# Moving the S5 and merge arithmetic of a two-layer diffusion trunk from GpSimd to VectorE, with branch products in their own PSUM tile

## The chip, the cores and the metric

The kernel runs on one core of one Trainium2 chip. The metric is the device time of one execution in microseconds; the median of three runs of the kernel before is 2266.82 us (2264.76 to 2268.28).

The engines are named as in the profile: PE is TensorE's matmul, PEld its weight load, DVE is VectorE, ACT is ScalarE, POOL is GpSimd, SP is SyncE, whose queue issues all DMAs of this kernel.

## What is computed

Two layers over 512 latent tokens and 256 context tokens, width 1024. Each layer normalises its input, projects it with one wide matrix, feeds four mixers, and merges them:

```python
hx = _rmsnorm(x, p["norm_g"]) * (1.0 + scale_x) + shift_x
zx = _project(hx, p["w_in"], ALL_NAMES)
# four mixers: S5 (complex diagonal scan, GLU), short convolution,
# neighbourhood attention, grouped-query attention
for k, (name, y) in enumerate(zip(BRANCH_NAMES, ys)):
    gated = y * jax.nn.silu(z[name + "_gate"])
    contrib = jax.nn.sigmoid(z["merge_" + name]) * (gated @ p["w_br"][k])
    out = contrib if out is None else out + contrib
x_new = x + gate_x * (out @ p["w_out"])
```

The first layer carries context and latent tokens (768 columns, in the code two parts, "c" of 256 and "l" of 512); the second layer's outputs are wanted for the 512 latent tokens alone. The S5 mixer has 32 groups of 16 channels, 64 complex states each, run forwards and backwards.

## The kernel before

Activations lie with features on the 128 partitions and tokens along the free dimension. A dense product (`dense`, line 187) splits weights and activations into a rounded high part and a low rest, and makes three matmuls per tile: high by high, high by low, low by high. `unit` (line 164) loads a weight unit of 128x1024, casts the high parts on ACT (line 177) and subtracts for the low parts (line 178); `lo_eng` gives that subtraction to POOL and DVE in turn. Raw weights have 2 buffers, high and low halves 4 each, which is two units.

Each layer has two stages. `front` weaves attention tiles with projections, the convolution and gates. `back` merges the branches in the order convolution, neighbourhood attention, grouped-query attention, S5. In `merge`, for each of 8 output tiles m of a branch, `merge_z` makes the sigmoid's product (8 k-tiles) and its tanh (line 1293, tile `mt`, 3 buffers in layer one and 2 in layer two), and a second `dense` makes the branch's product from `gh` and `gl` (4 k-tiles), the gated branch output reloaded from DRAM (line 1304). DVE combines both (line 1325); POOL adds the result to the accumulator (lines 1330, 1327). Both products use the PSUM tiles `pl` (2 buffers) and `pc` (1 buffer). The sigmoid of m+1 is emitted ahead of the branch product of m.

During the first three merges `tick` emits the S5 work of 8 blocks of 4 groups from a plan with due times (`s5_plan`). A block has:

- `s5_factors`: from a table of powers (`skl`) and the layer's matrices it makes `sX` (six small operations, lines 1012 to 1017), and per direction `swin` on DVE (512 columns) and `sWO` on POOL (576 columns), each of three operations at lines 1030 to 1032
- `s5_phases` (layer one only): six operations on 768 columns, lines 965 to 970; ACT negates the result at line 971
- `s5_matrices`: transposes and small products on PE (lines 1049, 1058)
- `s5_states`: a rotation (lines 1143 to 1145, two products and an add), the scan (1147), a rotation back (1150, 1151) and differences (1155 to 1158). Before each rotation the halves are swapped by DMAs (lines 1141, 1148). One of the two products is on POOL (1144, 1151)
- `s5_outputs` on PE (lines 1173 to 1175)

During the S5 merge and the output products of layer one, `s5_ahead` makes the factors and matrices of the first `n_ahead // 4` blocks of layer two, stores them to DRAM, and layer two loads them. The rest is made in layer two.

Instructions of each engine run in the order that the scheduler wrote them in at build time: by priority, which is program order except for weight units and attention tiles, and by when its own model of time has them ready. So later work can stand ahead of earlier work that waits.

Of the kernel before, what the change touches and what calls it, by code (L numbers as in the profile page):

```python
# [11 lines left out]
F32 = mybir.dt.float32  # L12
# [25 lines left out]
SG = 4  # L38
# [84 lines left out]
class Net:  # L123
# [63 lines left out]
    def dense(self, w, k0, nk, xh, xl, parts, base=0, turn=0):  # L187
# [485 lines left out]
    def front(self, l, pool, parts):  # L673

        self.attention_constants(pool)
# [109 lines left out]
    K_PR, K_PI, K_BR, K_AR, K_BI, K_AI, K_FR, K_FI, K_RHO, K_N = 0, 9, 18, 26, 38, 46, 58, 59, 60, 61  # L785
    NE = 2 * SG

    def s5_prep(self, pool):
# [147 lines left out]
        self.pd = self.tc.dram_tile([32 // SG, 128, self.K_N * self.NE], F32, name="pd")  # L936
        for c in range(32 // SG):
            R = pool.tile([128, self.K_N, self.NE], F32, name="skt", bufs=2)
            e = slice(c * self.NE, (c + 1) * self.NE)
            for col, t, w in ((self.K_PR, pr, 9), (self.K_PI, pi, 9), (self.K_FR, fr, 1), (self.K_FI, fi, 1), (self.K_RHO, rho, 1),  # L940
                              (self.K_BR, br_, 8), (self.K_BI, bi_, 8), (self.K_AR, ar_, 12), (self.K_AI, ai_, 12)):
                nc.scalar.copy(R[:, col:col + w], t[:, :w, e] if w > 1 else t[:, None, e])
            nc.sync.dma_start(self.pd[c], R.rearrange("p k e -> p (k e)"))
# [3 lines left out]
    def s5_table(self, l, pool, g0):  # L947

        K = pool.tile([128, self.K_N, self.NE], F32, name="skl", bufs=2)
        for h in range(2):  # L950
            self.nc.sync.dma_start(K[64 * h:64 * h + 64].rearrange("p k e -> p (k e)"), self.pd[g0 // SG][64 * l:64 * l + 64])
        return K

    def s5_phases(self, pool, prep, g0):
# [4 lines left out]
        P = prep.tile([128, self.K_N, self.NE], F32, name="skl", bufs=2)  # L959
        nc.sync.dma_start(P.rearrange("p k e -> p (k e)"), self.pd[g0 // SG])  # L960
# [31 lines left out]
    def s5_factors(self, l, pool, out, g0, bufs):  # L992
# [3 lines left out]
        P = self.s5_table(l, pool, g0)  # L996
# [13 lines left out]
        fr, fi = (P[:, c, :, None].to_broadcast([128, self.NE, 16]) for c in (self.K_FR, self.K_FI))  # L1010
# [8 lines left out]
        def powered(out, d, k0, k1, desc, m1, m2, w):  # L1019

            E = V if w == 8 else G

# [427 lines left out]
```

## Time and profile before

| | us |
|---|---|
| median of 3 runs | 2266.82 |
| the profiled execution, whole | 2275.09 |
| its span, first to last instruction | 2273.3 |
| PE busy | 2132.0 (94%) |
| DVE busy | 1308.9 (58%) |
| ACT busy | 891.7 (39%) |
| POOL busy | 818.7 (36%) |

The profiled execution is 8.3 us over the median of the runs. The stages, read from the lines at work: front of layer one to about 678 us, back of layer one to about 1300, front of layer two to about 1837, back of layer two to the end. A busy share says nothing of which wait ends last; the rows below are read by stage, and of each wait the releaser is named. PEclk is the share of TensorE's full clock that was granted: 1.0 is 2.4 GHz, and 0.5, its only other level here, 1.2 GHz.

### The profile page before, as it was taken

The numbers are of one execution on the slowest core, as the hardware profiler recorded it, in microseconds if no ns is written. First come the engines' busy times: TensorE is split into PE (matmuls) and PEld (weight loads), VectorE is DVE, ScalarE is ACT, GpSimd is POOL, SyncE is SP. The second block draws the span as 40 slices with busy tenths as digits, with TensorE's granted clock in tenths as the row PEclk, the third lists the DMA queues.
The fourth block names the chain that finished last, engine by engine and source line by source line (L and its number), as shares of the span: only waits on it lengthen the run. The fifth ranks groups of instructions, "written<-read, shape, count | busy, mean of one in ns | idle before, by whom it ended". The sixth has DMA issues, their size and how long they took to land.

```text
span 2273.3 us, 34769 instructions
## 1 busy us (share of the span) xinstructions
PE 2132.0 (94%) x12868; PEld 1817.7 (80%) x12868; DVE 1308.9 (58%) x2466; ACT 891.7 (39%) x1936; POOL 818.7 (36%) x630
## 2 busy tenths in 40 slices
PE   8999999999997989989999999999999979888999
PEld 3788888888986877778887897888788868777877
DVE  6477675688647667865337533555446644465322
ACT  3454454446442322222334235555445533223332
POOL 1712122222314436554247423222323333474332
PEclk9999999999998989999999989999999989988999
DMA  6454454433225453453255635444423357644344
GB/s 243 126 154 131 113 174 130 129 102 103 95 87 163 136 163 107 127 168 107 67 191 167 203 119 193 110 121 124 142 84 105 96 144 208 199 121 132 122 130 138
DMA packets 163470, 310.94 MB, mean 137 GB/s; under 512 B 58594, under 2 KB 82402, under 8 KB 162532
## 3 DMA queue, kind: packets, MB, share of 16 engines
q1 hardware_dynamic: 163300, 308.72, 44.8%
q8 instruction: 101, 1.65, 0.3%
q14 instruction: 69, 0.57, 0.1%
HBM read 211.33 MB, written 48.55 MB: 114 GB/s over the span
## 4 chain that ended last, share of the span: by engine, by line
PE 43%; DVE 6%; DMA 5%; issue 3%; SPq 3%; POOL 2%; ACT 1%; DVEq 0%; ACTq 0%; POOLq 0%
PE pl L204 29%; PE pc L204 5%; PE M L594 2%; DMA s<-s 1%; PE T L585 1%; DMA gl<-gd 1%; SPq L1067 1%; PE T L1058 1%; PE S L558 1%; DMA s<-yd 1%; PE S L560 1%; PE M L473 1%; DVE swin L1030 0%; DMA gd<-s 0%; PE T L1132 0%
## 5 line engine op out<-in xcount | busy, mean ns | idle before, releaser
L204 PE MATMUL pl<-hh,whi 128*128 128x512 f32 x1312 | 533.1, 408 | 23.1 <-ACT whi L177 10.1
L204 PE MATMUL pl<-hh,wlo 128*128 128x512 f32 x1312 | 531.0, 405 | 11.0 <-DVE wlo L178 6.5
L178 POOL TENSOR_TENSOR wlo<-wraw,whi 128x512 fp32r<-128x512 f32 x220 | 311.6, 1420 | 636.3 <-ACT whi L177 555.7
L204 PE MATMUL pl<-hl,whi 128*128 128x512 f32 x1312 | 531.2, 405 | 0.0
L177 ACT CAST whi<-wraw 128x512 fp32r<-128x512 f32 x440 | 271.3, 619 | 541.7 <-PE pl L204 242.5
L204 PEld LDWEIGHTS pl<-hh,whi 128*128 128x128 f32 x1312 | 253.8, 194 | 76.9 <-ACT whi L177 11.0
L204 PEld LDWEIGHTS pl<-hh,wlo 128*128 128x128 f32 x1312 | 252.9, 193 | 67.3 <-DVE wlo L178 8.5
L204 PEld LDWEIGHTS pl<-hl,whi 128*128 128x128 f32 x1312 | 253.6, 193 | 51.9 <-DVE hl L225 0.6
L178 DVE TENSOR_TENSOR wlo<-wraw,whi 128x512 fp32r<-128x512 f32 x220 | 181.8, 829 | 163.6 <-ACT whi L177 162.7
L204 PE MATMUL pc<-hh,whi 128*128 128x256 f32 x768 | 227.2, 296 | 13.8 <-DVE mt L1325 5.8
L204 PE MATMUL pc<-hl,whi 128*128 128x256 f32 x768 | 223.5, 291 | 0.8 <-DVE hl L225 0.8
L204 PE MATMUL pc<-hh,wlo 128*128 128x256 f32 x768 | 222.5, 290 | 0.0
L204 PEld LDWEIGHTS pc<-hh,whi 128*128 128x128 f32 x768 | 149.9, 195 | 23.2 <-DVE mt L1325 6.7
L574 ACT ACTIVATE s<-s,stiny 128x512 f32<-128x512 f32 (+2 forms) x160 | 112.5, 703 | 111.9 <-DVE stiny L573 55.7
L204 PEld LDWEIGHTS pc<-hl,whi 128*128 128x128 f32 x768 | 149.9, 195 | 5.8 <-DVE hl L225 1.8
L204 PEld LDWEIGHTS pc<-hh,wlo 128*128 128x128 f32 x768 | 149.9, 195 | 0.3
L594 PE MATMUL M<-ph,v 128*64 128x128 f32 x1216 | 146.3, 227 | 3.3 <-ACT y L612 1.4
L204 PE MATMUL pl<-gh,whi 128*128 128x512 f32 x256 | 106.3, 415 | 31.0 <-DMA gh<-gd 20.1
L594 PEld LDWEIGHTS M<-ph,v 128*64 128x64 f32 x1216 | 126.3, 137 | 10.9 <-ACT y L612 2.8
L224 ACT CAST ph<-T 128x512 fp32r<-128x512 f32 (+2 forms) x192 | 92.6, 496 | 57.0 <-PE T L585 50.0
L479 POOL TENSOR_TENSOR qtiny<-qtiny,kc 128x12 f32<-128x12 f32 (+1 forms) x26 | 56.0, 2155 | 140.3 <-DVE qtiny L477 113.0
L204 PE MATMUL pl<-gl,whi 128*128 128x512 f32 x256 | 104.2, 407 | 2.4 <-DMA gl<-gd 2.4
(785 smaller groups left out, 4230.9 us busy)
## 6 DMA issues: line engine op xcount, KB each, us to landing
wraw<-wu SPq DMA_DIRECT2D x220, 512.0 KB
wada<-wada SPq DMA_DIRECT2D x40, 512.0 KB
s<-s SPq DMA_DIRECT2D x80, 192.0 KB
bias<-bias SPq DMA_DIRECT2D x64, 128.0 KB
kh<-qhi SPq DMA_DIRECT2D x40, 192.0 KB
kl<-qlo SPq DMA_DIRECT2D x40, 192.0 KB
gh<-gd SPq DMA_DIRECT2D x16, 384.0 KB
gl<-gd SPq DMA_DIRECT2D x16, 384.0 KB
```

The costliest lines, as they stand in the source:

```text
L177: nc.scalar.copy(hi, raw[:, c])
L178: e.tensor_tensor(lo, raw[:, c], hi.bitcast(F32), op=OP.subtract)
L204: mm = nc.tensor.matmul(out[q], a[:, c], b[k][:, s], start=k + n == 0, stop=k == nk - 1 and n == 2)
L224: self.nc.scalar.copy(hi, src)
L473: nc.tensor.matmul(sums[:, 2 * b:2 * b + 2], sq[:, c:c + 128], self.blk1, start=True, stop=True)
L479: nc.gpsimd.tensor_tensor(r[:, :2 * nb], t[:, :2 * nb], self.mhalf.to_broadcast([128, 2 * nb]), op=OP.pow)
L558: nc.tensor.matmul(S[:, 512 - n:512], qa, k[:, CTX + k0 * 64:CTX + k0 * 64 + n], start=i == 0, stop=i == 1)
L560: nc.tensor.matmul(S[:, 512:768], qa, k[:, :CTX], start=i == 0, stop=i == 1)
L574: nc.scalar.activation(s[:, a:e], s[:, a:e], AF.Exp, bias=tn[:, 1:2], accum_out=tn[:, 2:3])
L585: nc.tensor.transpose(T[:, (b - b0) * 128:(b - b0 + 1) * 128], s[:, a + b * 128:a + (b + 1) * 128], self.ident)
L594: last = nc.tensor.matmul(o[:64, :128], v[:, vb, w], p[:, c], start=i == 0, stop=i == 3 * nb - 1)
L1058: nc.tensor.matmul(o[:16, g * 128:(g + 1) * 128], X[:, 0, d, g], WO[:, d, g, d:d + 8].rearrange("p k i -> p (k i)"), start=True, stop=True)
```

## The change

- `lo_eng` gives the low halves to POOL and DVE in turn only in the front stages; in the back stages all go to DVE.
- `sWO`, the second product of both S5 rotations, and the accumulator's adds go from POOL to DVE.
- The table of powers lies per column with the powers contiguous, so that an operation reads them at a step of one element and not of eight; the radius column goes to its end.
- The branch product of `merge` goes to the PSUM tile `S` (1024 columns, one buffer), which the attention tiles use in the front stages.
- The sigmoids come from one list for all branches, and up to three are held. Of the S5 branch only the first may come before its merge starts.
- `n_ahead` is 32: all 8 blocks of layer two are made in layer one.
- In layer two `mt` has 3 buffers, `gh` and `gl` have 2, and the pool for making weights is gone.

```diff
     @property
     def lo_eng(self):
         self._n = getattr(self, "_n", 0) + 1
-        return self.nc.gpsimd if self._n % 2 else self.nc.vector
+        return self.nc.gpsimd if self._n % 2 and self.in_front else self.nc.vector
...
-                if q not in out:
+                if wide is not None:
+                    out[q] = wide[:, 512:512 + s.stop - s.start] if q == "c" else wide[:, :512]
+                elif q not in out:
...
-        A = lambda c: P[:, c:c + 12].rearrange("p a e -> p e a")[:, :, :, None].to_broadcast([128, self.NE, 12, 8])
-        B = lambda c: P[:, c:c + 8].rearrange("p b e -> p e b")[:, :, None, :].to_broadcast([128, self.NE, 12, 8])
+        A = lambda c: P[:, :, c:c + 12, None].to_broadcast([128, self.NE, 12, 8])
+        B = lambda c: P[:, :, None, c:c + 8].to_broadcast([128, self.NE, 12, 8])
...
-            E = V if w == 8 else G
...
-            E.tensor_tensor(out, pw(self.K_PR), mm(m1), op=OP.mult)
-            E.tensor_tensor(tp, pw(self.K_PI), mm(m2), op=OP.mult)
-            E.tensor_tensor(out, out, tp, op=OP.add)
+            V.tensor_tensor(out, pw(self.K_PR), mm(m1), op=OP.mult)
+            V.tensor_tensor(tp, pw(self.K_PI), mm(m2), op=OP.mult)
+            V.tensor_tensor(out, out, tp, op=OP.add)
...
-        G.tensor_tensor(xs, xs, S, op=OP.mult)
+        V.tensor_tensor(xs, xs, S, op=OP.mult)
...
-        G.tensor_tensor(gs, gs, S, op=OP.mult)
+        V.tensor_tensor(gs, gs, S, op=OP.mult)
...
-    n_ahead = 24
+    n_ahead = 32
...
-            if (br, m) not in self.mz:
-                self.merge_z(l, br, m, parts)
-            if m < 7:
-                self.merge_z(l, br, m + 1, parts)
-            elif after is not None:
-                self.merge_z(l, after, 0, parts)
+            ahead = [x for x in self.zs if x[0] != B_S5 or x[1] == 0 or br == B_S5]
+            for x in ahead[:max(0, 3 - len(self.mz))]:
+                self.zs.remove(x)
+                self.merge_z(l, *x, parts)
...
-            b = self.dense(w, 4 * (m % 2), 4, gh, gl, parts, self.base)
+            wide = self.ps.tile([128, 1024], F32, name="S")
+            b = self.dense(w, 4 * (m % 2), 4, gh, gl, parts, self.base, wide=wide)
...
-                nc.gpsimd.tensor_tensor(t, acc[m], t, op=OP.add)
+                nc.vector.tensor_tensor(t, acc[m], t, op=OP.add)
...
-                nc.gpsimd.tensor_tensor(acc[m], acc[m], t, op=OP.add)
+                nc.vector.tensor_tensor(acc[m], acc[m], t, op=OP.add)
...
+            self.ngh = 2 if last else 1
+            prep = None if last else stack.enter_context(tc.tile_pool(name=f"s5p_{l}", bufs=1, reuse_waits="tile"))
...
-                net.nmt, net.mz = (3, 2)[l], {}
+                net.nmt, net.mz = 3, {}
```

## Rows read from the trace of the kernel before

**Rows 1.** Busy time by stretch, the two back stages; columns: window, length, engines, PEclk, DMA
```profile
678.50:1300.00 621.50, 566.39 (x3273) 486.33 (x3273) 390.90 (x467) 183.36 (x358) 301.80 (x202) 0.95 0.49 145
...
1837.40:2273.30 435.90, 392.16 (x1793) 319.51 (x1792) 189.46 (x223) 126.65 (x234) 180.74 (x135) 0.95 0.51 152
```

**Rows 2.** The same view, finer: the first back stage's start and its S5 blocks
```profile
678.50:700.00 21.50, 8.91 (x30) 7.12 (x30) 14.76 (x13) 2.51 (x6) 8.98 (x7) 0.68 0.78 259
700.00:1100.00 400.00, 364.10 (x2111) 313.84 (x2110) 267.75 (x311) 114.22 (x225) 191.90 (x130) 0.94 0.47 131
```

**Rows 3.** Waits of PE, first back stage: us in total, times, longest
```profile
PE pl L204 <- DMA gh<-gd: 12.6, 1, 12.6
PE pl L204 <- ACT whi L177: 10.1, 3, 4.5
PE T L1174 <- DVE s L1155: 6.8, 2, 3.8
PE pc L204 <- DVE mt L1325: 5.8, 2, 5.1
```

**Rows 4.** Waits of PE, second back stage
```profile
PE T L1058 <- POOL sWO L1032: 10.2, 2, 5.6
PE pl L204 <- DMA gh<-gd: 7.5, 2, 6.4
PE pl L204 <- ACT mt L1293: 7.0, 3, 4.5
PE pl L204 <- DVE acc L1325: 6.0, 1, 6.0
```

**Rows 5.** PE in order of time: start and duration, us
```profile
676.28 0.40 PE L204 MATMUL pl<-hh,whi 128*128 128x512 f32 x1
676.51 0.39 PE L204 MATMUL pl<-hl,whi 128*128 128x512 f32 x1
...
677.09 0.28 PE L204 MATMUL pc<-hl,whi 128*128 128x256 f32 x1
677.21 0.27 PE L204 MATMUL pc<-hh,wlo 128*128 128x256 f32 x1
...
860.40 1.92 PE L1058 MATMUL T<-sWO,sX 128*16 128x128 f32 x16
```

**Rows 6.** SP's queue in order of time, start of the first back stage
```profile
680.34 1.11 SPq L951 DMA_DIRECT2D skl<-pd  x2
...
687.12 0.43 SPq L1304 DMA_DIRECT2D gh<-gd  x1
```

**Rows 7.** Lines of the first back stage: duration ns min/median/max, first and last start
```profile
L178 DVE TENSOR_TENSOR wlo<-wraw,whi x55: 659/692/2366, 679.2 to 1298.1; 128x512 fp32r<-128x512 f32 x55
...
L1325 DVE SCALAR_TENSOR_TENSOR mt<-mt,pl x24: 653/680/689, 848.1 to 1274.7; 128x512 f32<-128x512 f32 x24
...
L1030 DVE TENSOR_TENSOR swin<-skl,sX x28: 672/678/1785, 688.0 to 1271.1; 128x512 f32<-128x512 f32 x28
...
L1016 DVE TENSOR_TENSOR sXt<-smt,skl x14: 273/288/1462, 686.9 to 1268.2; 128x128 f32<-128x128 f32 x14
...
L965 DVE TENSOR_TENSOR s<-skl x8: 1655/1686/3324, 694.4 to 1013.2; 128x768 f32<-128x768 f32 x8
...
L970 DVE TENSOR_TENSOR s<-s,s x8: 935/944/961, 704.6 to 1026.5; 128x768 f32<-128x768 f32 x8
...
L1144 POOL TENSOR_TENSOR s<-s,s x8: 2180/2599/6022, 735.2 to 1059.8; 128x768 f32<-128x768 f32 x8
```

**Rows 8.** A group of the first back stage by form: busy us, mean ns, idle before
```profile
L178 DVE TENSOR_TENSOR wlo<-wraw,whi 128x512 fp32r<-128x512 f32 x55 | 55.2, 1007 | 50.1 <-ACT whi L177 49.6
```

**Rows 9.** Other engines' waits, first back stage
```profile
ACT s L971 <- DVE s L970: 29.5, 5, 8.0
...
POOL wlo L178 <- ACT whi L177: 99.9, 22, 14.1
```

**Rows 10.** Second back stage, a group by form that waits for a swap by DMA
```profile
L1143 DVE TENSOR_TENSOR s<-s,sC 128x768 f32<-128x768 f32 x8 | 8.2, 1023 | 42.8 <-DMA s<-s 41.2 <-ACT whi L177 1.7
```

More of the change, by code (lines that the diff above doesn't have):

```diff
@@ L935, in s5_prep @@
         yield from powers(ar_, ai_, 1, 11)
[L936 removed]
+        self.pd = self.tc.dram_tile([32 // SG, 128, self.K_ALL], F32, name="pd")
         for c in range(32 // SG):
[L938 removed]
+            R = pool.tile([128, self.K_ALL], F32, name="skt", bufs=2)
             e = slice(c * self.NE, (c + 1) * self.NE)
[L940 removed]
+            for col, t, w in ((self.K_PR, pr, 9), (self.K_PI, pi, 9), (self.K_FR, fr, 1), (self.K_FI, fi, 1),
                               (self.K_BR, br_, 8), (self.K_BI, bi_, 8), (self.K_AR, ar_, 12), (self.K_AI, ai_, 12)):
[L942 to L943 removed]
+                nc.scalar.copy(self.s5_cols(R)[:, :, col:col + w], t[:, :w, e].rearrange("p k e -> p e k") if w > 1 else t[:, e, None])
+            nc.scalar.copy(R[:, self.NE * self.K_N:], rho[:, e])
+            nc.sync.dma_start(self.pd[c], R)
             if c % 2:
@@ L947, in s5_table @@
     def s5_table(self, l, pool, g0):
-        K = pool.tile([128, self.K_N, self.NE], F32, name="skl", bufs=2)
+        K = pool.tile([128, self.K_ALL], F32, name="skl", bufs=2)
         for h in range(2):
-            self.nc.sync.dma_start(K[64 * h:64 * h + 64].rearrange("p k e -> p (k e)"), self.pd[g0 // SG][64 * l:64 * l + 64])
+            self.nc.sync.dma_start(K[64 * h:64 * h + 64], self.pd[g0 // SG][64 * l:64 * l + 64])
         return K
@@ L1009, in s5_factors @@
         nc.scalar.activation(f2(3), f2(3), AF.Copy, scale=-1.0)
-        fr, fi = (P[:, c, :, None].to_broadcast([128, self.NE, 16]) for c in (self.K_FR, self.K_FI))
+        fr, fi = (P[:, :, c:c + 1].to_broadcast([128, self.NE, 16]) for c in (self.K_FR, self.K_FI))
         e3 = lambda t: t.rearrange("p d g i -> p (d g) i")
@@ L1294, in merge_z, with merge @@
         self.mz[br, m] = t
-    def merge(self, l, pool, br, parts, acc, done=None, after=None):
+    def merge(self, l, pool, br, parts, acc, done=None):
         nc = self.nc
@@ L1336, in back @@
         sp = self.span(parts)
+        self.in_front = False
         with ExitStack() as stack:
@@ L1341, in merges @@
             def merges():
-                for br, after in ((B_CONV, B_NA), (B_NA, B_GQA), (B_GQA, B_S5)):
-                    yield from self.merge(l, pm, br, parts, acc, None, after)
+                for br in (B_CONV, B_NA, B_GQA):
+                    yield from self.merge(l, pm, br, parts, acc)
+            self.zs = [(br, m) for br in (B_CONV, B_NA, B_GQA, B_S5) for m in range(8)]
             last = l == L - 1
-            prep = stack.enter_context(tc.tile_pool(name=f"s5p_{l}", bufs=1, reuse_waits="tile"))
+            self.ngh = 2 if last else 1
+            prep = None if last else stack.enter_context(tc.tile_pool(name=f"s5p_{l}", bufs=1, reuse_waits="tile"))
             ahead = iter(()) if last else self.s5_ahead(l + 1, prep)
```

31 lines of the change are left out of this document (19 added, 12 removed).

## The prediction

> **What bounds the kernel now.** I read the page first, then the busy time by stretch, then PE's waits in the two stretches that the change touches, and last the lines of the engines that release them. TensorE sets the time: over the two back stages it is busy 566.4 of 621.5 us and 392.2 of 435.9 us [rows 1]. So nothing is gained by making VectorE or GpSimd cheaper as such. What can be gained is PE's idle time, 55.1 us in the first back stage and 43.7 us in the second, and what the lower clock takes. The granted share is 0.95 in both [rows 1], which is 31 and 22 us of full-speed pulses not granted; those that fell into idle time cost nothing. The half-speed spells stand with the gaps: 0.68 in the 21.5 us that hold the longest gap, 0.94 over the S5 blocks [rows 2]. The front stages run the same code before and after but for a few table copies on ACT at the end of the first; I count them as zero, and their own drift as 5 us either way.
>
> The reader should then see in the waits that few gaps are the S5 arithmetic itself. The first stage's four largest are 12.6 us for `gh` from DRAM, 10.1 us for weight casts on ACT, 6.8 us for the S5 outputs' state, and 5.8 us in which a sigmoid's product waits for `pc` until VectorE has read the branch product before it [rows 3]. The second stage's are 10.2 us for `sWO` on POOL, 7.5 us for `gh`, 7.0 us for a tanh that has not freed `pl`, and 6.0 us for VectorE's read of a branch product [rows 4].
>
> **The price of a product.** Successive 512-column matmuls start 0.23 us apart, 256-column ones 0.12 us [rows 5]. A sigmoid's product in layer one is 24 of each, 8.4 us; a branch product is half, 4.2 us. In layer two, without context, they are 5.5 and 2.8 us.
>
> **Sigmoids ahead.** The S5 loads of the plan's first moment go out on SP from 680.3 us, the eight `gh` and `gl` loads only from 687.1 us [rows 6], and PE, with its two sigmoid products done, waits 12.6 us. A third product of 8.4 us now stands in front, independent of these loads. It needs one more weight unit, for which two units of buffers are there. The gap shrinks to about 4 us, and the half clock of that stretch (0.32 x 21.5 = 6.9 us of pulses, most of them under the idle) gives a few more: I take 11 of the 12.6 and what the clock adds to it (ends 8 and 16). The same at the second layer's start: 5.5 us of product against a longest wait of 6.4 [rows 4], so I take 5. At the later branch borders there is still one product between the last branch product and the reload, so nothing changes there; the second `gh` buffer of layer two covers little that PE waits for, 1.1 us.
>
> **Branch products in `S`.** Before, each product needs the one `pc` that the product before it left, so a late read by VectorE stops the next sigmoid: 5.8 us [rows 3], all of it gone, since sigmoids now follow only on ACT's read of the sigmoid before. In layer two `pl` alternated between the two kinds, and a tanh had 2.8 us to free it; now two sigmoids lie apart by 11 us. I take 6 of the 7.0 us. In the other direction `S` has one buffer. Between two branch products stands mostly a sigmoid's product, 8.4 or 5.5 us, against a read of 0.68 us [rows 7], plus 0.42 for the context part. But with the sigmoids early, the last products of the grouped-query and S5 branches run back to back: three times per layer PE waits for the read, about 1.3 us in layer one and 0.9 in layer two: a loss of 4 and 3 us, if VectorE is not behind.
>
> **Arithmetic on VectorE.** In the first back stage it takes 54 half-unit splits (0.69 us), 84 `sWO` operations (estimate 0.76 us, 576 columns from 512 at 0.68), 24 accumulator adds and 16 rotations (0.95 us by the 768-column row): 37 + 64 + 23 + 15 = 139 us [rows 7]. The two further blocks of weights add 2 x (6 x 0.29 + 6 x 0.68 + 6 x 0.76) = 21 us [rows 7].
>
> Against that, the four phase operations with the table's strided reads take 1.69 us where the same 768 columns, contiguous, take 0.94 [rows 7]: with contiguous powers I take 0.95, 32 x 0.74 = 24 us less (ends 0 and 24). And operations with two inputs in SBUF stretch while POOL works: the split's median is 0.69 us and its longest 2.37, and 55 of them take 55.2 us, 17 more than their median gives [rows 7, 8]; the branch read, whose second input is PSUM, stays between 0.65 and 0.69 [rows 7]. With POOL silent I expect all at their medians, and over all lines I take 65 us less (ends 17, the splits alone, and 100). So VectorE's load goes from 391 us to about 391 + 139 + 21 - 24 - 65 = 462 us of 600: higher, not full.
>
> The Trainium skill says, in "SBUF — State Buffer", Who interferes with whom, that a VectorE instruction with two SBUF inputs and a GpSimd one that reads SBUF shut each other out for the whole instruction. The two rows of line 178 and line 1325 agree with it; by it alone all of the stretch would go.
>
> On the path this shows in three places. The weight casts that PE waits for stand behind ACT's line 971, which waits 29.5 us for the end of the phases [rows 9]; phases that take 4 x 0.74 us less, uncontended, should give 5 of the 10.1 us. The rotation's second product takes 2.6 us on POOL [rows 7] and 0.95 behind the first on VectorE, so each of a block's two rotations ends about 0.7 us sooner: 3 of the 6.8 us. Of the 19.8 us of smaller waits in this stage I take 5. In the second stage 3 of the 6.0 us for the read, and 3 of the 13 us of smaller ones.
>
> **All weights made early.** Layer two loses its two makings, and the 10.2 us for `sWO` go, with about 3 us of clock. Layer one gets them where it is tight. Per output tile of the S5 merge VectorE now has 10.4 (weights) + 0.4 + 3 x 0.69 (splits) + 1.1 (read) + 0.95 (add) + 0.95 (low part) = 15.9 us. PE has 8.4 + 4.2 + about 3.1 for the matrices (1.92 us for their 16 small products [rows 5], an estimate of 1.2 for the eight transposes) = 15.7 us. This is even until the sigmoids run out; then PE has 7.3 us per tile for two tiles and VectorE 15.9, and the reads that free `S` stand behind the weights. That is up to 2 x 8.6 = 17 us, less what the output products, which need neither, fill in: I take 10 (ends 0 and 25), and 2 of clock.
>
> **The sum.** First stage: 11 + 6 (`pc`) + 5 + 3 + 5, less 4, 10 and 2, is 14. Clock over the S5 blocks: 0.06 x 400 = 24 us not granted beside 36 us of idle [rows 2]; with half of this idle gone I take 7. So 21. Second: 5 + 13 + 6 + 3 + 3, and 3 of clock, less 3, is 30. Together 51 us. The profiled execution's 2275 us becomes 2224; it lies 8.3 us above the median of the runs, against which the sum is 2216. Some stalls now hidden will come to the surface: I give back 4 and forecast **2220 us**, with a range of its own from 2195 to 2250.
>
> **Rivals.** (a) *More is freed.* If real order and written order agree once nothing is stretched, most gaps go. Idle of 98.8 us and some 25 us of costly half clock are there; three quarters of that, less the new stalls, is 75 to 90 us: 2184. For it: gaps are many and small. Against: waits for DMA stay.
>
> (b) *The gain is returned at the S5 merge.* VectorE at 15.9 us per tile against 15.7 has no slack, and any in-order wait adds. At the upper end the new stall is 25 us and clock 8, and half of the other gains fail: 2258.
>
> (c) *VectorE's queue becomes the stall, slower.* All splits now stand in one queue with the S5 chain. POOL waited 99.9 us for casts [rows 9], and these waits go to VectorE; it already waits 41.2 us for swaps in layer two [rows 10]. It decides once a split falls more than PE's lead of one unit (8.4 or 5.5 us) behind: a swap's wait, 41.2/8 = 5.2 us in the mean for the first of each block [rows 10], comes near to that. If each of the 32 swaps of both layers holds PE for half of this, 2.6 us, 83 us stand against the 51 and the 10 of (b)'s kind that come anyway: about 2290. For it: the lead is short. Against: POOL's half was queued behind the same swaps before. The Trainium skill ("TensorE: Matmul & The Clock Gate", the table at its head) calls VectorE's queue strictly first in, first out; the waits above agree, and it is what this rival needs.
>
> (d) *The stretch is not POOL's doing* and stays: VectorE then needs about 391 + 160 x 1.007/0.692 - 24 = 600 of 621 us [rows 7, 8], and the S5 merge 15.9 x 1.46 = 23 us per tile against PE's 15.7, 58 us over eight tiles; near 2300.
>
> **How the numbers follow.** Forecast 0.55, (a) 0.15, (b) 0.14, (c) 0.12, (d) 0.04. About 0.2% is what a measurement of this kernel can tell from no change, 4.5 us. Faster: the forecast, (a) and half of (b), 0.77; same, the other part of (b), 0.07; slower 0.16. The range of 2180 to 2268 leaves out (c), (d) and a little below.
>
> **What would show it.** No gap above 5 us before the first `gh` product of either layer; no wait of a sigmoid on line 1325; line 178 on VectorE at 0.69 us throughout, lines 965 to 969 at 0.95; no weights made after 1840 us; a VectorE near full, and PE waiting for `S`, at the end of the S5 merge of layer one. Wrong would be: PE waiting for `wlo` on VectorE in many places (c), or half-clock spells in new gaps at the S5 merge (b).

## The result and the profile after

The changed kernel takes 2166.47 us (median of four runs, 2164.21 to 2171.66) against 2265.79 us before; the ratio is 0.9569, with a 95% interval of 0.9542 to 0.9595. The profiled execution is one of 2171.66 us with a span of 2169.9. So the gain is 99 us where 51 were summed, and the time lies below both ranges that the prediction names; it is even 18 us below rival (a), "more is freed". Where the 103 us between the two spans come from is seen in the two back stages. To cut them alike in both traces, take each from the first tanh of a sigmoid (line 1293 before, 1304 after) to the layer's last residual addition (lines 1376 and 1389). The second stretch runs on to the end of the trace, 3 us after the last addition.

Busy time by stretch, before (window, length, PE, PEld, DVE, ACT, POOL, PEclk, DMA share, GB/s):

```profile
668.10:1362.40 694.30, 639.19 (x3698) 552.01 (x3697) 412.50 (x497) 208.45 (x403) 324.44 (x219) 0.95 0.48 142
1826.10:2273.30 447.20, 403.46 (x1894) 329.67 (x1892) 192.40 (x228) 131.12 (x245) 182.01 (x136) 0.95 0.50 151
```

The same stretches after:

```profile
670.90:1303.90 633.00, 619.96 (x3737) 538.52 (x3736) 437.78 (x723) 216.63 (x417) 10.27 (x30) 0.98 0.54 162
1771.90:2169.90 398.00, 384.52 (x1846) 315.50 (x1844) 204.18 (x299) 125.01 (x231) 3.33 (x25) 0.99 0.55 172
```

Length less busy is PE's idle time: 55.1 us become 13.0, and 43.7 become 13.5, together 72. The busy time itself falls by 19.2 and 18.9 us, together 38, although the same products are made (the small ones of two S5 blocks have moved from the second stage to the first). That is the clock, whose share rises from 0.95 to 0.98 and 0.99. 61 us and 49 us are gained in the back stages, and the fronts give back 7. So nearly three quarters of the idle time and most of the half clock went. One new stall came for them, the first line below, which is not among the waits of the kernel before.

What is left of PE's waits in the first back stage (us in total, times, longest), to be read against [rows 3]:

```profile
PE pl L209 <- ACT s L229: 7.5, 1, 7.5
PE T L1185 <- DVE s L1166: 2.6, 1, 2.6
PE S L209 <- DVE mt L1335: 1.6, 1, 1.6
PE S L209 <- DMA gh<-gd: 0.6, 1, 0.6
```

And in the second, against [rows 4]:

```profile
PE pl L209 <- DVE wlo L178: 6.1, 3, 3.7
PE S L209 <- DMA gl<-gd: 1.6, 2, 1.4
PE S L209 <- DVE acc L1335: 0.8, 1, 0.8
```

The 12.6 us for `gh` are 0.6, the 10.1 us for weight casts and the waits for `pc` are gone, and so are `sWO`, `gh` and the tanh of layer two. VectorE's operations are back at their shortest (duration ns min/median/max; [rows 7] has 659/692/2366 and, for the phases, 1655/1686/3324):

```profile
L178 DVE TENSOR_TENSOR wlo<-wraw,whi x128: 667/686/706, 671.1 to 1296.8; 128x512 fp32r<-128x512 f32 x128
...
L977 DVE TENSOR_TENSOR s<-skl x8: 949/951/953, 693.7 to 986.7; 128x768 f32<-128x768 f32 x8
```

In the first back stage VectorE is busy for 438 us, only 25 more than before, although GpSimd's busy time has gone from 324 us to 10 and the weights of two more blocks are made there.

### The profile page after: what moved, and what is told of

Its sections match the earlier page's. It is cut to its first block, busy times and chain, and to the rows that moved or that the text cites. A ratio compares the mean times of both kernels' runs of the same rounds, so it can differ in the third digit from the quotient of the medians.

```text
span 2169.9 us, 34654 instructions
## 1 busy us (share of the span) xinstructions
PE 2097.1 (97%) x12868; PEld 1792.5 (83%) x12868; DVE 1351.5 (62%) x2770; ACT 898.5 (41%) x1936; POOL 322.3 (15%) x326
## 4 chain that ended last, share of the span: by engine, by line
PE 65%; DMA 6%; DVE 5%; ACT 2%; SPq 1%; issue 1%; POOL 0%; DVEq 0%; ACTq 0%; POOLq 0%
PE pl L209 34%; PE pc L209 10%; PE S L209 8%; PE M L599 3%; DMA s<-s 2%; PE T L590 2%; PE T L1069 1%; PE S L563 1%; PE S L565 1%; PE T L1143 1%; DMA gl<-gd 1%; DMA gd<-s 1%; PE M L478 1%; PE T L1060 1%; DMA s<-yd 1%
## 5 line engine op out<-in xcount | busy, mean ns | idle before, releaser
L209 PE MATMUL pl<-hh,whi 128*128 128x512 f32 x1312 | 526.5, 403 | 5.4 <-ACT hh L229 2.5
L209 PE MATMUL pl<-hh,wlo 128*128 128x512 f32 x1312 | 525.3, 400 | 6.1 <-DVE wlo L178 6.1
L209 PE MATMUL pl<-hl,whi 128*128 128x512 f32 x1312 | 525.0, 400 | 0.4 <-DVE hl L230 0.4
L178 DVE TENSOR_TENSOR wlo<-wraw,whi 128x512 fp32r<-128x512 f32 x348 | 241.4, 696 | 185.0 <-ACT whi L177 178.1
L178 POOL TENSOR_TENSOR wlo<-wraw,whi 128x512 fp32r<-128x512 f32 x92 | 128.0, 1394 | 314.0 <-ACT whi L177 273.5
L209 PE MATMUL S<-gh,whi 128*128 128x512 f32 (+1 forms) x384 | 139.0, 362 | 3.0 <-DVE mt L1335 1.6
L209 PE MATMUL S<-gl,whi 128*128 128x512 f32 (+1 forms) x384 | 137.5, 358 | 1.6 <-DMA gl<-gd 1.6
L209 PE MATMUL S<-gh,wlo 128*128 128x512 f32 (+1 forms) x384 | 137.2, 357 | 0.0
```

The source lines that it names most:

```text
L178: e.tensor_tensor(lo, raw[:, c], hi.bitcast(F32), op=OP.subtract)
L209: mm = nc.tensor.matmul(out[q], a[:, c], b[k][:, s], start=k + n == 0, stop=k == nk - 1 and n == 2)
```

## The experiments

Times are medians; the kernel before lies between 2264.6 and 2269.0 us beside them, and the changed kernel at 2166.5 in its own comparison.

**Which part brought it.** Theory A: GpSimd's tensor work was the cause. Theory B: PSUM tile and sigmoids decouple PE, and GpSimd matters little. Each of the first four runs undoes one part of the change. (In the edits shown, `...` stands for lines left out.) First GpSimd's work:

```diff
-        return self.nc.gpsimd if self._n % 2 and self.in_front else self.nc.vector
+        return self.nc.gpsimd if self._n % 2 else self.nc.vector
...
+            E = V if w == 8 else G
...
-        V.tensor_tensor(xs, xs, S, op=OP.mult)
+        G.tensor_tensor(xs, xs, S, op=OP.mult)
...
-                nc.vector.tensor_tensor(acc[m], acc[m], t, op=OP.add)
+                nc.gpsimd.tensor_tensor(acc[m], acc[m], t, op=OP.add)
```

> The changed kernel with its tensor work on GpSimd again as before: every second low half in the back stages, sWO, the rotations' second products, the accumulator's adds. Theory A (most of the 99 us comes from GpSimd's tensor work: stretched operations and a second in-order queue put the real order out of step with the written one, and PE's many small gaps and half-clock spells follow): 2225 to 2245 us, both back stages lose 25 to 40 us each, wlo on VectorE back at a mean near 1.0 us against 0.69. Theory B (the PSUM tile and the sigmoids ahead decouple PE, and GpSimd matters little): 2170 to 2190 us, the stretched wlo is back but PE's gaps are not.

Measured: 2246.93 us, ratio 0.9908 (0.9884 to 0.9932). Of the 99 us only 19 to 21 are left; the time is 2 us above theory A's range. Theory A had expected a loss of 25 to 40 us in each back stage. Of the two, shown below, the first is 69 us longer than in the changed kernel, and longer than before; the second loses 13 us and keeps most of its gain:

```profile
666.40:1368.20 701.80, 646.12 (x3742) 559.53 (x3741) 415.24 (x526) 216.14 (x422) 325.66 (x231) 0.95 0.48 147
1834.60:2245.40 410.80, 391.04 (x1846) 320.07 (x1844) 173.09 (x200) 124.86 (x231) 155.76 (x124) 0.98 0.53 167
```

In the first back stage PE waits now for the S5 states instead of weight casts:

```profile
PE T L1186 <- DVE s L1167: 29.0, 7, 5.9
PE T L1061 <- DVE swin L1044: 9.7, 7, 3.9
PE T L1187 <- DVE s L1170: 5.5, 6, 2.6
```

These are other names than in [rows 3], for a stage of about the same length: the delay is about the same, and where it surfaces has changed with the order.

Next, the branch products go back to `pl` and `pc`, with one sigmoid ahead:

```diff
-            ahead = [x for x in self.zs if x[0] != B_S5 or x[1] == 0 or br == B_S5]
-            for x in ahead[:max(0, 3 - len(self.mz))]:
+            if (br, m) not in self.mz:
+                self.merge_z(l, br, m, parts)
...
-            b = self.dense(w, 4 * (m % 2), 4, gh, gl, parts, self.base, wide=wide)
+            b = self.dense(w, 4 * (m % 2), 4, gh, gl, parts, self.base)
```

> The changed kernel with branch products in pl and pc again and one sigmoid ahead instead of two. Theory A: 2180 to 2195 us; what comes back is the start of both back stages (12.6 and 6 us of gap before) and a few us of pc. Theory B: 2215 to 2240 us, with waits for pc and pl spread over both back stages. My prediction's own price for this part is 11 + 5 + 6 + 6 less 7, 21 us, that is 2187 us.

Measured: 2186.78 us, 0.9643 (0.9617 to 0.9669), 20 us more than the changed kernel, against the prediction's price of 21. The waits are those that it named, but the shares are not: in the traces the first back stage is 10 us longer and the second 19, where the price was 13 and 8. First back stage, then second:

```profile
PE pl L209 <- DMA gh<-gd: 17.4, 4, 13.1
```

```profile
PE pl L209 <- DMA gh<-gd: 9.5, 3, 6.4
PE pl L209 <- DVE wlo L178: 6.3, 4, 3.0
PE pl L209 <- ACT mt L1304: 4.9, 2, 4.3
PE pl L209 <- DVE acc L1335: 3.4, 1, 3.4
```

Next, the table of powers is laid out as before (one of the lines):

```diff
-        A = lambda c: P[:, :, c:c + 12, None].to_broadcast([128, self.NE, 12, 8])
+        A = lambda c: P[:, c:c + 12].rearrange("p a e -> p e a")[:, :, :, None].to_broadcast([128, self.NE, 12, 8])
```

> The changed kernel with the table of powers laid out as before, powers 8 elements apart. The four phase operations go back from 0.95 to 1.69 us, 24 us of VectorE in the first back stage. Theory A and theory B alike: this is off PE's path, 2166 to 2174 us. If VectorE's in-order queue is near the path there, as the prediction had it (5 us for the casts behind the phases): 2172 to 2182 us.

Measured: 2174.56 us, 0.9588 (0.9562 to 0.9615). The phases take 1.63 to 1.67 us again, 23 us in all of VectorE. That is 8 us more by the medians, half a us above the range of both theories and inside the one in which VectorE's queue is near the path. But the interval overlaps that of the changed kernel, so the 8 us are not told apart from nothing.

Last, two blocks of layer two are made there again (`n_ahead`):

```diff
-    n_ahead = 32
+    n_ahead = 24
...
-            self.ngh = 2 if last else 1
-            prep = None if last else stack.enter_context(...)
+            self.ngh = 1
+            prep = stack.enter_context(...)
```

> The changed kernel with n_ahead 24 again: two of layer two's blocks are made in layer two, on VectorE, and the pool for it is there; one gh buffer. The prediction priced this at 10 + 3 us in layer two less 12 us in layer one, so 2168 us by it. Theory A: the 10.2 us gap before came of sWO on slow GpSimd, so on VectorE it costs less: 2166 to 2174 us. If making the weights inside layer two is itself the stall: 2176 to 2190 us, all of it after 1790 us.

Measured: 2172.37 us, 0.9577 (0.9545 to 0.9609), not told apart from the changed kernel. In the traces the second back stage is 10 us longer, the first 3 us shorter.

Then the opposite, one part alone on the kernel before:

```diff
-        return self.nc.gpsimd if self._n % 2 else self.nc.vector
+        return self.nc.gpsimd if self._n % 2 and self.in_front else self.nc.vector
...
-            E = V if w == 8 else G
+            E = V
...
-        G.tensor_tensor(xs, xs, S, op=OP.mult)
+        V.tensor_tensor(xs, xs, S, op=OP.mult)
...
```

> The kernel before with only the move to VectorE: split halves of the back stages, sWO, rotations, accumulator adds; table, PSUM tiles, sigmoid order and n_ahead as before. If the parts add as the runs that undo one each say (20 us for PSUM and sigmoids, 4 to 8 for the table, about 4 for n_ahead): 2187 to 2202 us, with 13 us of gap at the first back stage's start and 6 at the second's still there. By the prediction's price for this part (5 + 3 + 5 + 3 + 3 + 3 us and some clock, about 30): about 2237 us.

Measured: 2197.77 us, 0.9688 (0.9651 to 0.9726): 67 us from the move alone. The first back stage is 49 us shorter than before (645), the second 30 (418). The longest wait is the 12.2 us for `gh` at the start, as expected:

```profile
PE pl L206 <- DMA gh<-gd: 12.6, 3, 12.2
```

67 and the 20, 8 and 6 of the other parts make 101 of the 99, though the 8 and the 6 are not told apart from nothing. Theory A holds.

**Stretch, or GpSimd's own slowness.** The move does two things: it silences GpSimd's reads (A1), and it takes slow steps off the S5 chain and a second queue (A2). To tell them apart, GpSimd gets work that nobody waits for:

```diff
             elif not first:
                 nc.vector.tensor_tensor(acc[m], acc[m], t, op=OP.add)
+            if not done:
+                j = pool.tile([128, 512], F32, name="junk", bufs=1)
+                s4 = acc[m][:, :512]
+                nc.gpsimd.tensor_tensor(j[:, :1], s4[:, :1], s4[:, :1], op=OP.mult)
+                for _ in range(7 if 'c' in parts else 4):
+                    nc.gpsimd.tensor_tensor(j, s4, s4, op=OP.mult)
```

> The changed kernel, and after each branch product of the first three merges GpSimd multiplies half an accumulator tile by itself into a tile that nobody reads: 7 times 512 columns in layer one, 4 in layer two, some 250 to 300 us of GpSimd's time. Nobody waits for it, and the order on TensorE, VectorE and ScalarE is that of the changed kernel but for a few steps. Theory A1 (GpSimd hurts by the stretch of VectorE's two-input operations alone): wlo's mean back to 0.9 to 1.1 us, 2205 to 2240 us. Theory A2 (it hurt because it is slow itself and in line: the rotations' products of 2.5 us, sWO of 4.5 us, its queue): VectorE may stretch, but the time stays at 2166 to 2185 us.

and, as the control, with writes in place of the reads:

```diff
-                for _ in range(7 if 'c' in parts else 4):
-                    nc.gpsimd.tensor_tensor(j, s4, s4, op=OP.mult)
+                for _ in range(14 if 'c' in parts else 8):
+                    nc.gpsimd.memset(j, 0.0)
```

> The control for the run with idle reads: the same program on the other engines, but GpSimd only writes constants into that tile, 14 and 8 times 512 columns, and reads one column. Theory A1: nothing is stretched that has two inputs in SBUF, wlo's mean stays at 0.69 to 0.72 us, 2166 to 2176 us. If any use of SBUF by GpSimd stretches VectorE, it comes near to the run with reads.

Measured: 2250.23 us with reads (0.9939, 0.9916 to 0.9963), 10 us above A1's range, and 2163.81 with writes (0.9550, 0.9532 to 0.9568). The instructions of PE, VectorE and ScalarE and their order are the same in both; GpSimd is busy in both. 86 us lie between them. Its queue is not the cause: the only work behind the idle reads that others need are small memsets of the S5 states, and in each of the 16 blocks these end at least 4.9 us before the VectorE difference (line 1166) that PE waits for. The two back stages, with reads:

```profile
665.80:1368.80 703.00, 647.39 (x3737) 560.23 (x3736) 524.43 (x723) 214.94 (x417) 265.55 (x222) 0.94 0.48 146
1833.10:2248.40 415.30, 390.16 (x1846) 318.93 (x1844) 237.95 (x299) 124.23 (x231) 132.25 (x145) 0.98 0.54 165
```

and with writes:

```profile
660.40:1294.10 633.70, 621.66 (x3736) 539.82 (x3736) 438.07 (x723) 216.36 (x417) 208.09 (x390) 0.98 0.54 162
1763.20:2158.70 395.50, 382.74 (x1846) 314.65 (x1844) 204.38 (x299) 124.83 (x231) 113.65 (x241) 1.00 0.55 173
```

The same 723 VectorE instructions take 524 us or 438. VectorE in order of time with reads (start, us), from the third line on beside three reads:

```profile
730.82 1.00 DVE L1335 SCALAR_TENSOR_TENSOR acc<-mt,S 128x256 f32<-128x256 f32 x2
731.75 0.68 DVE L178 TENSOR_TENSOR wlo<-wraw,whi 128x512 fp32r<-128x512 f32 x1
732.35 1.79 DVE L981 TENSOR_TENSOR s<-skl 128x768 f32<-128x768 f32 x1
734.06 1.79 DVE L1156 TENSOR_TENSOR s<-s,s 128x768 f32<-128x768 f32 x1
735.78 1.52 DVE L1042 TENSOR_TENSOR spw<-skl,sX 128x512 f32<-128x512 f32 x1
```

GpSimd in that time:

```profile
731.97 4.79 POOL L1346 TENSOR_TENSOR junk<-acc 128x512 f32<-128x512 f32 x3 [0.41 <-DVE acc L1335]
```

The same steps in the changed kernel:

```profile
726.62 1.01 DVE L1335 SCALAR_TENSOR_TENSOR acc<-mt,S 128x256 f32<-128x256 f32 x2
727.55 0.69 DVE L178 TENSOR_TENSOR wlo<-wraw,whi 128x512 fp32r<-128x512 f32 x1
728.16 0.95 DVE L981 TENSOR_TENSOR s<-skl 128x768 f32<-128x768 f32 x1
729.02 0.95 DVE L1156 TENSOR_TENSOR s<-s,s 128x768 f32<-128x768 f32 x1
729.89 0.69 DVE L1042 TENSOR_TENSOR spw<-skl,sX 128x512 f32<-128x512 f32 x1
```

0.95 becomes 1.79 and 0.69 becomes 1.52: a VectorE operation that is held up by a read is longer by the same 0.84 us, whatever its size, and the three reads, 1.04 us at the shortest, take 1.6 each. Three and three take turns. A line of 128 columns, 267 to 294 ns in the changed kernel, shows the same step with reads:

```profile
L1026 DVE TENSOR_TENSOR sXt<-smt,skl x8: 264/690/1122, 707.2 to 1058.5; 128x128 f32<-128x128 f32 x8
```

Not each meeting costs that: of the 170 `tensor_tensor` operations of VectorE that overlap a read by more than 0.1 us between 690 and 1060 us, 72 are longer by 0.83 to 0.88 us and 68 by less than 0.05. The branch read, with one input in PSUM, isn't longer in any case (394/546/683 in the changed kernel):

```profile
L1335 DVE SCALAR_TENSOR_TENSOR mt<-mt,S x48: 391/546/683, 848.3 to 1281.8; 128x256 f32<-128x256 f32 x24, 128x512 f32<-128x512 f32 x24
```

The Trainium skill ("SBUF — State Buffer", Who interferes with whom) states that a VectorE operation with two SBUF inputs contends with a GpSimd one that reads SBUF, and not with one that only writes it; both runs agree. PE's waits with reads, first back stage:

```profile
PE T L1185 <- DVE s L1166: 22.0, 6, 5.0
PE pl L209 <- DVE wlo L178: 9.7, 2, 5.5
```

So A1: stretch alone brings back as much as all of GpSimd's work did (84 us against 80). That shows that stretch is enough. It does not show that GpSimd's own slowness cost nothing in the kernel before: with all its work back, ACT waits 27.0 us in the first back stage for GpSimd's adds (line 1338), and how much of this reaches PE stays open.

**How much stretch it takes.** Parts of GpSimd's work, alone and in pairs, and fewer idle reads. The rotations alone:

```diff
-        V.tensor_tensor(xs, xs, S, op=OP.mult)
+        G.tensor_tensor(xs, xs, S, op=OP.mult)
...
-        V.tensor_tensor(gs, gs, S, op=OP.mult)
+        G.tensor_tensor(gs, gs, S, op=OP.mult)
```

> The changed kernel with only the second products of the two S5 rotations on GpSimd (32 operations of 768 columns, 2.5 us each beside VectorE). Theory A2: the chain of the states is late for the output products again, most of the 80 us that giving back all of GpSimd's work cost: 2200 to 2235 us. Theory A1: GpSimd is busy for 80 us of 1000, little stretch: 2170 to 2182 us. By the prediction's own price (0.7 us for a rotation, 3 us in all): 2170 us.

The split halves alone:

```diff
-        return self.nc.gpsimd if self._n % 2 and self.in_front else self.nc.vector
+        return self.nc.gpsimd if self._n % 2 else self.nc.vector
```

> The changed kernel with only every second low half of the back stages on GpSimd (some 100 operations of 512 columns, 1.4 to 1.6 us each). Theory A1: some 150 us of GpSimd reads, mostly beside VectorE's work, so a third to a half of the 80 us: 2190 to 2210 us. Theory A2: PE's lead is a unit, and 1.5 us for a half does not use it up: 2166 to 2180 us.

Measured: 2159.64 us (0.9536, 0.9516 to 0.9556) and 2160.74 us (0.9538, 0.9521 to 0.9555): neither costs anything. Neither theory fits both runs. For the rotations A2 had expected 2200 to 2235 us and A1 2170 to 2182, for the splits A1 2190 to 2210 and A2 2166 to 2180. The splits are 64 halves and 115 us of GpSimd's time in the first back stage, with no loss. So the slow steps of the rotations did not set the time, and the cost isn't proportional to the reads. Next, 3 and 2 idle reads in place of 7 and 4; splits and rotations together (the two edits above); and `sWO` alone:

```diff
-                for _ in range(7 if 'c' in parts else 4):
+                for _ in range(3 if 'c' in parts else 2):
```

> The kernel with idle reads, with 3 of them (layer one) and 2 (layer two) in place of 7 and 4; the program of the other engines is the same. Theory O (a VectorE and a GpSimd operation that both read SBUF exclude each other, and the time is lost once the two together fill the stage): 72 reads of 1.04 us beside VectorE's 285 us in the 402 us of the S5 blocks are 360, so there is room: 2164 to 2180 us, wlo's mean 0.72 to 0.76 us. Theory L (each microsecond of reads costs its share): 40 per cent of the 84 us, 2195 to 2205 us.

> The changed kernel with both the split halves and the rotations' second products on GpSimd, each of which alone cost nothing. GpSimd was busy 81 and 53 us of the 402 us of the S5 blocks in those two, VectorE would have some 250 of its own. Theory O: 380 of 402 us, at the edge: 2165 to 2195 us. Theory L, which adds what each cost alone: 2155 to 2166 us.

```diff
+            E = V if w == 8 else G
...
-            V.tensor_tensor(out, pw(self.K_PR), mm(m1), op=OP.mult)
+            E.tensor_tensor(out, pw(self.K_PR), mm(m1), op=OP.mult)
```

> The changed kernel with only sWO on GpSimd (three operations of 576 columns in a row, 4.5 us). Theory O: some 85 us of GpSimd and 235 of VectorE in the 402 us of the S5 blocks, 320, so there is room: 2158 to 2172 us. Theory Q (what cost the time was this one long block in GpSimd's queue, since the other two parts alone cost nothing): 2190 to 2230 us.

Measured: 2190.75 us (0.9656, 0.9619 to 0.9692), 2178.50 us (0.9603, 0.9562 to 0.9644) and 2163.76 us (0.9534, 0.9496 to 0.9572). Theory Q (the long block) falls with the last. The fewer idle reads cost 24 us, which is above theory O's range and just below L's; the splits and rotations together lie in O's range and above L's. All runs by what happens in the stretch from 690 to 1040 us, the S5 blocks (stretch: over all groups of VectorE instructions of one line and shape, the sum of the durations less count times the shortest; stages from one trace each, times are medians). Two of the rows that the second column is read from, changed kernel and idle reads:

```profile
690.00:1040.00 350.00, 345.23 (x2124) 302.15 (x2122) 265.74 (x429) 113.95 (x224) 2.31 (x24) 1.00 0.56 160
690.00:1040.00 350.00, 315.38 (x1810) 273.93 (x1809) 297.13 (x360) 96.54 (x192) 208.80 (x169) 0.93 0.47 138
```

| kernel | DVE + POOL busy, of 350 us | stretch | first back stage | time |
|---|---|---|---|---|
| changed | 266 + 2 | 4 | 633 | 2166 |
| rotations back | 265 + 53 | 18 | 625 | 2160 |
| splits back | 260 + 74 | 20 | 631 | 2161 |
| sWO back | 249 + 63 | 22 | 635 | 2164 |
| splits and rotations back | 258 + 101 | 37 | 641 | 2179 |
| fewer idle reads | 288 + 121 | 41 | 653 | 2191 |
| before | 251 + 178 | 66 | 694 | 2266 |
| all of GpSimd's work back | 234 + 163 | 70 | 702 | 2247 |
| idle reads | 297 + 209 | 79 | 703 | 2250 |

Up to some 22 us of stretch in 350 nothing is lost; at 37 to 41 the stage is 8 to 20 us longer, at 70 and 79 by 69 and 70. (The kernel before, with 66 and 61, lacks the other parts of the change too.) Where the stretch falls counts as well: over the whole stage the splits have 42 us of it and `sWO` 65 and lose nothing, and the fewer idle reads with 47 lose 20. In the second back stage 35 to 39 us of stretch cost only 13 to 17. The busy times together tell nearly the same, with the turn where they reach the stretch's length (334 free, 359 not), but the run with all work back (397) loses more than the one with fewer reads (409); the count isn't exact.

**Why a VectorE that isn't full costs that much.** Under the idle reads VectorE is busy for 85% of these 350 us. Theory W: PE waits because VectorE has less time. Theory P: because the order was written without knowing of the stretch. So VectorE gets as much extra work as the stretch was, but known when the order is written:

```diff
+            if not done:
+                j = pool.tile([128, 512], F32, name="junk", bufs=1)
+                s4 = acc[m][:, :512]
+                for _ in range(5 if 'c' in parts else 2):
+                    nc.vector.tensor_tensor(j, s4, s4, op=OP.mult)
```

> The changed kernel, and after each branch product of the first three merges VectorE itself makes 5 (layer one) or 2 (layer two) idle multiplications of 512 columns, 0.69 us each: 82 and 33 us more of VectorE's time, about as much as the idle GpSimd reads cost it in stretch (79 us over the S5 blocks, 98 over the stage, 39 in layer two), but known when the order was written. Theory W (PE waits because VectorE has that much less time): 2225 to 2250 us, as with the reads. Theory P (stretch costs because the written order does not know of it, so that short steps fall behind long ones): 2166 to 2185 us.

Measured: 2182.47 us, 0.9632 (0.9605 to 0.9659): 16 us, not 84. The first back stage:

```profile
662.30:1317.20 654.90, 625.07 (x3744) 542.49 (x3742) 512.44 (x846) 218.95 (x421) 11.69 (x31) 0.96 0.53 157
```

VectorE is busy for 512 us here and for 524 under the reads (from 690 to 1040 us for 324 and 297), and the stage takes 655 us against 703. PE's idle time is 30 us, and two single waits make 20 of it:

```profile
PE T L1184 <- DMA sTT<-sln: 10.8, 1, 10.8
PE T L1185 <- DVE s L1166: 8.9, 1, 8.9
```

W falls as the main cause. What stays open is whether P is the whole of it: stretch is unplanned, but it also comes in bunches (three operations in a row above lose 2.5 us), while the planned work was mostly spread out (109 of its 131 runs are single operations). No run here separates the two.

**The same in the fronts, and a faster kernel.** GpSimd still reads in the front stages. First the low halves of the fronts go to VectorE:

```diff
-        return self.nc.gpsimd if self._n % 2 and self.in_front else self.nc.vector
+        return self.nc.vector
```

> The changed kernel with the front stages' low halves on VectorE too: 83 operations of 1.3 to 1.4 us go from GpSimd, which keeps 130 us of other work there. Where the two engines' times together stay within the stretch (457 + 181 of 676 us, 230 + 106 of 414), stretch cost nothing in the back stages, so by this: 2160 to 2172 us, no change. If any stretch costs PE time in the fronts: 2145 to 2158 us.

Measured: 2140.04 us, 0.9440 (0.9415 to 0.9465), 26 us less than the changed kernel and below both ranges. The busy-time count, by which the fronts had room, was wrong here. Fronts of the changed kernel, then of this one:

```profile
0.00:670.90 670.90, 638.30 (x4293) 545.46 (x4294) 455.22 (x1172) 320.12 (x778) 180.75 (x152) 0.96 0.42 132
1303.90:1771.90 468.00, 454.33 (x2997) 393.02 (x2996) 254.32 (x578) 236.75 (x513) 127.94 (x120) 0.98 0.40 121
```

```profile
0.00:645.70 645.70, 622.77 (x4293) 535.60 (x4294) 459.95 (x1218) 320.60 (x778) 116.66 (x106) 0.97 0.43 137
1281.00:1732.80 451.80, 446.27 (x2991) 388.25 (x2990) 275.17 (x619) 234.84 (x512) 67.41 (x75) 0.99 0.41 125
```

VectorE takes GpSimd's splits of the first front, some 46, and is busy only 5 us longer; idle time and PE's busy time both fall. These two traces lie further apart than the medians (36 us); in the last kernel below, with the same front work, the fronts take 658 and 461 us, 20 less than in the changed kernel. Then the fronts' other products as well:

```diff
-        (nc.vector if k % 2 == 0 else nc.gpsimd).tensor_tensor(h, x, rs, op=OP.mult)
+        nc.vector.tensor_tensor(h, x, rs, op=OP.mult)
...
-            nc.gpsimd.tensor_tensor(t, t, y, op=OP.mult)
+            nc.vector.tensor_tensor(t, t, y, op=OP.mult)
...
-            nc.gpsimd.tensor_tensor(n[:, s], n[:, s], self.cos, op=OP.mult)
+            nc.vector.tensor_tensor(n[:, s], n[:, s], self.cos, op=OP.mult)
```

> The kernel with the front stages' split halves on VectorE, and now the gates' products, the rotary products and half of the norm's products of the fronts too (some 65 us of GpSimd's time); GpSimd keeps powers, one-column copies and constants. Theory P (stretch that the written order does not know of costs about its length, work that it knows of costs little): another 5 to 15 us, 2125 to 2137 us. If VectorE's load in the fronts is now what counts: 2138 to 2150 us.

Measured: 2148.32 us, 0.9477 (0.9447 to 0.9507): no further gain, by the medians 8 us worse (the intervals overlap a little). The stretch of the two fronts together is 75 us in the changed kernel, 46 with the splits on VectorE and 19 here: the first 29 us less brought 26 us, the next 27 brought nothing. The time lies in the range in which VectorE's load would count, but VectorE is busy here for 460 and 282 us of the fronts, against 460 and 275 with the splits alone. That all of GpSimd's work should go falls with this, and with it theory P in this form; why the last part brought nothing was not tried further. Last, the 7.5 us that PE waits before the S5 gates, which the changed kernel, the idle writes and the planned work all show. Two sigmoids of the S5 branch may come ahead instead of one:

```diff
-            ahead = [x for x in self.zs if x[0] != B_S5 or x[1] == 0 or br == B_S5]
+            ahead = [x for x in self.zs if x[0] != B_S5 or x[1] <= 1 or br == B_S5]
```

tried with the rotations on GpSimd, with all the fronts' products on VectorE, and with the fronts' splits alone:

> The kernel with only the rotations' second products on GpSimd, and two sigmoids of the S5 branch instead of one let ahead of the S5 gates, so that a product of 8.4 us stands where the changed kernel's TensorE waits 7.5 us for the high half of the S5 outputs. If that wait is on the path: 2150 to 2158 us. If the rotations alone had already taken it away by a change of order: 2156 to 2164 us.

> The same, and two sigmoids of the S5 branch let ahead of the S5 gates, which takes away the wait of 7.5 us before the gates: 6 us less than the run without it if the wait is there, no change if the order has filled it.

> The kernel with the front stages' split halves on VectorE (the other front work stays on GpSimd), and two sigmoids of the S5 branch let ahead of the S5 gates. With the other front work moved too, two ahead took 8 us; if that holds here, 2130 to 2136 us; if the wait before the gates is filled by a change of order already, 2138 to 2144 us.

Measured: 2162.28 us (0.9538, 0.9516 to 0.9560), no change, since the order there had no such wait; 2140.25 us (0.9445, 0.9418 to 0.9472), 8 us less by the medians; and 2133.44 us (0.9403, 0.9377 to 0.9429), by the medians 7 us less than without it, with intervals that overlap. The last is the fastest kernel of this study, 33 us below the changed one.

## Why the prediction was wrong

The sign, the place and the direction of nearly every step were right; the time was outside the range. The step that failed is the price of the arithmetic's move to VectorE: 24 us in the sum, 67 measured for the move alone. A second price was too small as well, that of the clock.

- **Sigmoids ahead and branch products in `S`** (11, 5, 6, 6, less 4 and 3: 21 us). Right in the sum and in the waits that were named: 20 us when undone, though more of it lies in the second stage than was said. No sigmoid waits for line 1335. Of the predicted waits for back-to-back reads, 1.6 and 0.8 us are seen.
- **The table** (0.95 us, 24 us of VectorE, 5 us on the path). Right in the operation (0.951); on the path 8 us by the medians, not told apart from nothing, so the 5 us are neither borne out nor refuted.
- **All weights made early** (13 us in layer two, 12 lost at the S5 merge). In the one trace the gain is 10 us. The loss didn't come: undoing it shortens the first back stage by 3 us, not 12. The sum per tile, 15.9 us of VectorE against 15.7, was made as if all eight blocks fell into the eight tiles of the merge. They don't; the makings of `sWO` run from 1117 to 1269 us, well into the output products:

```profile
L1041 DVE TENSOR_TENSOR sWO<-skl,smt x16: 750/752/759, 1116.8 to 1269.0; 128x576 f32<-128x576 f32 x16
```

In that time PE hardly pauses, and VectorE has a fifth free even in the fullest windows of 20 us, of which this is one:

```profile
1160.00:1180.00 20.00, 20.00 (x122) 16.88 (x120) 16.09 (x30) 8.69 (x19) 0.00 (x0) 1.00 0.61 186
```

- **Arithmetic on VectorE** (3, 5, 3 and 3 us of waits and 10 of clock: 24 us). Wrong: 67 us alone, 80 as the last part to be undone. The stretch was priced too low: 65 us less of VectorE, with ends 17 and 100, where the sum over the groups falls from 112 to 10 us in the first back stage (VectorE's load was to rise by 71 us, from 391 to 462; it rose by 25). Above all, what failed is how it was turned into PE's time. I looked for named waits and took a quarter to a half of each, 14 us in all. But the waits in which a delay surfaces change with the order ([rows 3], and the list with GpSimd's work back), so their names don't bound it. The whole stretch comes nearer: the move alone takes it from 66 us to 6 over the S5 blocks and the first back stage is 49 us shorter; with GpSimd's work back in the changed kernel it goes from 4 to 70, and the stage is 69 longer.
- **The clock** (7 and 3 us). Wrong in size: PE's busy time falls by 38 us. The S5 blocks ran at 0.94 [rows 2] and run at 0.98 now:

```profile
676.90:700.00 23.10, 23.10 (x139) 20.36 (x138) 13.37 (x23) 7.89 (x16) 1.95 (x2) 1.00 0.69 232
700.00:1060.00 360.00, 347.37 (x2116) 303.79 (x2115) 264.64 (x422) 115.92 (x225) 2.19 (x23) 0.98 0.53 149
```

The prediction wrote that half-speed spells stand with the gaps, and then counted 7 of the 24 us that they took over the S5 blocks. In these runs they went with the gaps.
- **The rivals.** (a) came nearest: real and written order agreeing again, which the run with planned work speaks for without settling it, had a chance of 0.15. It kept a quarter of the loss and still ended 18 us too high: the clock gave 38 us of busy time where (a) had some 25 in all. (b) and (c) did not happen: of the back stages' waits 6.1 us in layer two are for `wlo` on VectorE, none of any size in layer one. (d) fell: with GpSimd silent the split is at 0.69 us, and the run with idle reads brings the stretch back.

## What to carry to other kernels

When two engines lengthen each other's operations, price the effect as a whole: sum the durations over the shortest of each form in the stretch, and compare that with what the stage has been shown to absorb (here some 22 us in 350), instead of halving the waits in which it happens to surface. Beyond that, expect a loss that can be as large as the stretch itself, clock included, as in the first back stage (66 us more, 69 lost), but it need not be (31 us more, 13 lost in the second; nothing gained from the last 27 us in the fronts). A little work on the second engine is free; what costs is the sum, where the order is tight. And test such a cause with idle work that nobody waits for, with a control that differs in one property only.

## What was not expected of the hardware

- A GpSimd read that holds up VectorE costs it the same 0.84 us for a 512-column and a 768-column operation (0.69 to 1.52, 0.95 to 1.79); 128-column ones went from 0.28 to 1.12. What counts is how many are held up, not their size.
- An operation of VectorE with one tensor input is longer in the fronts as well while GpSimd has more to do (line 581, us busy and mean ns, first 640 us, changed kernel):

```profile
L581 DVE TENSOR_SCALAR s<-s,stiny 128x256 f32<-128x256 f32 x30 | 15.6, 518 | 0.5
```

and with the fronts' products on VectorE:

```profile
L581 DVE TENSOR_SCALAR s<-s,stiny 128x256 f32<-128x256 f32 x30 | 10.5, 351 | 0.5
```

The Trainium skill ("SBUF — State Buffer", Who interferes with whom) counts `tensor_scalar` among the operations that can take the ports shared with GpSimd; 518 against 351 ns agrees. The mean is 351 ns already with the splits alone on VectorE; no run changes GpSimd's reads and nothing else in the fronts.

- With a step of 32 bytes between the elements read a two-input operation of 768 columns takes 1.67 us (the run with the table as before), with contiguous ones 0.95 (the changed kernel).
